# Sums of weight blocks made by accumulating transfers, another order of products, and a branch's products held in DRAM

## The chip, the cores and the metric

The kernel runs on one core of one Trainium2 chip. The metric is the device time of one execution in microseconds (us); lower is better. The time of a kernel is the median of several runs. A profile is one further execution, recorded by the hardware profiler. The engines are named as the profile names them: PE (TensorE), PEld (its weight loads), DVE (VectorE), ACT (ScalarE), POOL (GpSimd) and SP (SyncE, which here only issues DMAs).

## What is computed

One layer of a hybrid encoder trunk on 512 tokens of width 1024, in float32. The core of the reference:

```python
h = _rmsnorm(x, g_pre_mix)
proj = h @ w_in
q, k, v, g, u, sv, a_ret, a_sgu = jnp.split(proj, ...)
y_ret = _retention_branch(q, k, v, g, ret_decay_logit, w_ret_o)     # (layernorm(o) * silu(g)) @ w_ret_o
y_sgu = _sgu_branch(u, sv, sgu_ln_g, sgu_ln_b, w_spatial, b_spatial, w_sgu_o)
merged = jax.nn.sigmoid(a_ret) * y_ret + jax.nn.sigmoid(a_sgu) * y_sgu
x = x + _rmsnorm(merged @ w_out, g_post_mix)
h2 = _rmsnorm(x, g_pre_ffn)
x = x + _rmsnorm(_conv_gated_mlp(h2, w_up, conv_w, conv_b, w_down), g_post_ffn)
```

`_conv_gated_mlp` is a product with `w_up` (1024 x 5632), a convolution over three tokens, a gate (gelu(a) * b) and a product with `w_down` (2816 x 1024).

## The kernel before, in words

**Weights.** All weights are laid out on the host as 146 blocks, `wall`, each 128 x 1024 float32 (512 KB). They stream through the chip in a fixed order of units. SP loads a block into a tile `raw` (a ring of four). Each float32 matrix is then split into two parts of a reduced format: ACT copies it to a high part (`copy`, L79) and DVE subtracts that to give a low part (`tensor_sub`, L86); both go into a ring `w4` of nine slots. PE makes each product as three: high by high, high by low, low by high. `w_get` hands out the next split block, and splits some units ahead (`LOOK`).

**Pairs.** Twenty pairs of blocks (four for `u`, eight for the two gates, eight in the up projection) are multiplied by a scheme with seven products instead of eight, in the manner of Strassen and Winograd. The four quarters of a pair's weight are B11, B12, B21 and B22, each 128 x 512. `w_form` makes the sums T1 = B11 + B12 (DVE, L167), T3 = B12 + B22 (DVE, L168), T2 = T1 + B22 (POOL, L169) and T4 = T2 + B21 (POOL, L171) in `raw` tiles. B12 itself takes part in no product. Each quarter or sum is one unit, split as above, in the order of `FORMS`. The class `Pair` makes the products of 12 matmuls of 128x256 each (L692) into three PSUM banks, b[0] to b[2]: `part1` multiplies B11 (bank 0), B21 (bank 1), T1 with S1 (bank 2) and T2 with S2 (bank 0 again), `part2` T3 with S3 (bank 0), `part3` T4 and B22. S1 to S4 are sums of activations. Where a bank is used again without being cleared, ACT has copied out (L79) or DVE has added what it held before. In the gates, whole blocks (`f_block`, 128x512 matmuls) lie between the parts.

**Down.** The down projection has two halves of nine units of a similar scheme, each with a block `q` (of which 768 columns are used as they are) and a block `t` made from `q`. `w_down` makes the first two columns of 256 of `t` by one DVE addition of a broadcast (L186), and two further ones by L190 and L191, then splits `t`. A pair `q`, `t` gives 42 matmuls of 128x256 (L1058); four whole blocks come between or behind (L1074).

**Stages.** The order on PE, with its time in the profiled execution: the input projections and the retention up to about 217 us; the four `u` pairs to 262 us; the eight gate pairs with whole blocks to 428 us, first four for the retention branch, then four for the SGU branch; the output projection `w_out` (two streamed blocks, then six resident ones, split ahead of use into tiles of their own), norms and transposes to about 500 us; up projection and convolution from 520 us (its first blocks begin before) to 706 us; down projection to the end at 825.7 us, with the last norms in the tail.

**Merging the gates.** For the retention branch `gated_pair` gives products that DVE multiplies by the gate into tiles `r`, eight in all, which stay in SBUF. For the SGU branch DVE multiplies likewise (L805), POOL adds `r` (L806), and the sum is split into `mh` and `ml`, the operands of `w_out`.

Engines work through their queues in order. What a scheduler decided beforehand is fixed in the program; the ring sizes (`raw` four, `w4` nine, `blk` 76 tiles of 128 x 512) say when a buffer may be filled again.

Of the kernel before, what the change touches and what calls it, by code (L numbers as in the profile page):

```python
# [26 lines left out]
NW = 146  # L27
U0, GATE0, GATE1 = 32, 40, 72
LOOK = 4
NBLK = 76  # L30
WARM = 18
RES_OUT = 6
DOWN0 = NW - NF
# [14 lines left out]
def tile_block(ctx: ExitStack, tc, xT, x, wall, par, cs, wsp, bsp, gpost, gffn, out):  # L48
    nc = tc.nc
    sb = ctx.enter_context(tc.tile_pool(name="sb", bufs=1))  # L50
    pp = ctx.enter_context(tc.tile_pool(name="pp", bufs=8, space=bass.MemoryType.PSUM))
    dp_ = ctx.enter_context(tc.tile_pool(name="dp", bufs=1, space=bass.MemoryType.DRAM))
# [3 lines left out]
    def nm(s):  # L56
        uid[0] += 1
        return f"{s}_{uid[0]}"

    def blk(dt=F32, n="blk", shape=(P, S)):  # L60
        return sb.tile(list(shape), dt, tag="blk", bufs=NBLK, name=nm(n))

# [15 lines left out]
    def copy(o, i):  # L78
        nc.scalar.activation(out=o, in_=i, func=AF.Copy)  # L79
# [4 lines left out]
    def split(hi, lo, src):  # L84
        copy(hi, src)
        nc.vector.tensor_sub(lo, src, as32(hi))  # L86
# [2 lines left out]

    RES1 = NW - 22 - 44  # L90
    RES0 = RES1 - RES_OUT
    FORMS = ("B11", "B21", "T1", "T2", "T3", "T4", "B22")
    units = []
    i = 0
    while i < NW:
        pair = [(f, i) for f in FORMS]
        if U0 <= i < GATE0:
            units += pair
            i += 2
        elif GATE0 <= i < GATE1:  # L100
            units += pair[:4] + [("blk", i + 2)] + pair[4:] + [("blk", i + 3)]
            i += 4
        elif i == UP0 + 2 * COUPLES[0][0]:
            for a, b in COUPLES:
                pair = [(f, UP0 + 2 * a) for f in FORMS]
                units += pair[:4] + [("blk", UP0 + 2 * b)] + pair[4:] + [("blk", UP0 + 2 * b + 1)]
            i = UP0 + 2 * COUPLES[-1][1] + 2
        elif i == DOWN0:
            for _ in range(2):
                pairs = [[("q", i + j), ("t", i + j)] for j in range(DP)]  # L110
                whole = [[("blk", i + DP)], [("blk", i + DP + 1)]]
                for u in pairs[:4] + whole[:1] + pairs[4:6] + whole[1:] + pairs[6:] if i == DOWN0 else pairs + whole:
                    units += u
                i += DP + WHOLE // 2
        else:
            units.append(("blk", i))
            i += 1
    w_ready, w_pos, w_held, w_raw = {}, [0, 0], [0], {}

    def raw_tile():  # L120
        return sb.tile([P, 1024], F32, tag="raw", bufs=4, name=nm("raw"))


    AT_64, AT_192 = 16, 48
# [31 lines left out]
    def w_form(form, i):  # L156

        if form == "B11":
            a, b = raw_tile(), raw_tile()
            nc.sync.dma_start(a, wall[i])  # L160
            nc.sync.dma_start(b, wall[i + 1])
            w_raw["B11"], w_raw["B12"] = a[:, :S], a[:, S:]
            w_raw["B22"], w_raw["B21"] = b[:, :S], b[:, S:]
        elif form == "T1":
            t = raw_tile()
            w_raw["T1"], w_raw["T2"], w_raw["T3"], w_raw["T4"] = t[:, :S], t[:, S:], w_raw["B12"], t[:, S:]
            nc.vector.tensor_add(w_raw["T1"], w_raw["B11"], w_raw["B12"])  # L167
            nc.vector.tensor_add(w_raw["T3"], w_raw["B12"], w_raw["B22"])  # L168
            nc.gpsimd.tensor_tensor(out=w_raw["T2"], in0=w_raw["T1"], in1=w_raw["B22"], op=ALU.add)  # L169
        elif form == "T4":  # L170
            nc.gpsimd.tensor_tensor(out=w_raw["T4"], in0=w_raw["T2"], in1=w_raw["B21"], op=ALU.add)  # L171
        w = slot("wf", 0, 1088)
        lo, hi = w[:, AT_64 : AT_64 + S], w[:, S + AT_192 : 2 * S + AT_192]
        split(hi, lo, w_raw[form])
        return hi, lo

    def w_down(form, i):

        if form == "q":
            raw = w_raw["q"] = raw_tile()  # L180
            nc.sync.dma_start(raw, wall[i])
            raw = raw[:, : 3 * 256]
        else:
            b, raw = w_raw["q"], raw_tile()
            two = "p (n c) -> p n c"
            nc.vector.tensor_tensor(  # L186
                out=raw[:, :512].rearrange(two, n=2), in0=b[:, :512].rearrange(two, n=2),
                in1=b[:, None, 768:].to_broadcast([P, 2, 256]), op=ALU.add,
            )
            nc.vector.tensor_add(raw[:, 512:768], raw[:, :256], b[:, 256:512])  # L190
            nc.vector.tensor_add(raw[:, 768:], raw[:, 512:768], b[:, 512:768])  # L191
        w = 768 if form == "q" else 1024
        hi, lo = slot("dh", AT_192, w), slot("dl", AT_192, w)
        split(hi, lo, raw)
        return hi, lo
# [70 lines left out]
    for k in range(KD):  # L266
# [18 lines left out]
        for m in range(8):  # L285
            c = slice(m * P, (m + 1) * P)
# [5 lines left out]
    T0, T1 = slice(0, 256), slice(256, 512)  # L292
# [383 lines left out]
    class Pair:  # L676
# [27 lines left out]
        def part1(self):  # L704
            c0, c1 = self.t
            o = self.product(0, self.x(0, T0), True)
            copy(c0[:, T0], o)
            o = self.product(1, self.x(4, T0), True)
            v.tensor_add(c0[:, T0], o, c0[:, T0])
            self.product(2, self.s("S1"), True)  # L710
            o = self.product(0, self.s("S2"), False)
            copy(c1[:, T0], o)
            if self.scale is not None:
                v.tensor_mul(c0[:, T0], c0[:, T0], self.scale[:, T0])

# [68 lines left out]
    def gated_pair(ah, al, late=None):  # L784
        p = Pair(AF.Sigmoid, lambda: tmp("sig"), None, rbc)
        p.part1()
        if late:
            late.part3()
        o = [f_block(ah, al, KD)]
        p.part2()  # L790
        o.append(f_block(ah, al, KD, p.part3))
        return zip(o, p.t)

    r = []
    for j in range(KD // 2):
        for o, t in gated_pair(ogh, ogl, late if j == 0 else None):
            b = blk(n="r")
            v.tensor_mul(b, o, t)
            r.append(b)
        mix(2 * j)  # L800
        mix(2 * j + 1)
    mh, ml = [], []
    for j in range(KD // 2):
        for i, (o, t) in enumerate(gated_pair(yh, yl)):
            v.tensor_mul(t, o, t)  # L805
            nc.gpsimd.tensor_tensor(out=t, in0=t, in1=r[2 * j + i], op=ALU.add)  # L806
            h_, l_ = blk(F32R, "mh"), blk(F32R, "ml")
            split(h_, l_, t)
            mh.append(h_)
            ml.append(l_)  # L810

    def bcast(src, n):
        t = halves(n)
        for i in range(2):
            nc.gpsimd.dma_start(t[i], src[None, i * S : (i + 1) * S].to_broadcast([P, S]))
        return t
# [229 lines left out]
    def products(m, j, steps={}, look=LOOK):  # L1046
        for n, (unit, at, act) in enumerate(UNITS):
            if n in (0, 3):
                wh, wl = w_get(look)
            if j == 0:  # L1050
                m[n] = ps()
            f = slice(at * 256, (at + 1) * 256)
            ah, al = dforms[j][act]
            for t in range(2):
                c = slice(t * P, (t + 1) * P)
                o = m[n][:, t * 256 : (t + 1) * 256]
                for i, (a_, w_) in enumerate(((ah, wh), (ah, wl), (al, wh))):
                    nc.tensor.matmul(  # L1058
                        o, a_[:, c], w_[:, f], start=j == t == i == 0,
                        stop=j == DP - 1 and i == 2 and n not in (M2, M3, M4), skip_group_check=True,  # L1060
                    )
            steps.get(n, lambda: None)()
# [17 lines left out]
    m = {}  # L1080
    m[M8] = ps()
    late = list(range(EAGER, DP))
    c11, c12, c21, c22 = c4 = [blk(n="c") for _ in range(4)]
    e1, e3, uu, yy = tmp("e1"), tmp("e3"), tmp("uu"), tmp("yy")

    def after6():
# [26 lines left out]
            if j == 5:  # L1113
                copy(c22, m[M8])

    gpf = bcast(gffn, "gpf")
    qn = [small("q", 4, 4) for _ in range(NT)]
    zg = []

# [71 lines left out]
    steps = {M1: lambda: copy(e1, m[M1]), M6: after6, M7: after7}  # L1191
    for j in range(DP):
        products(m, j, steps if j == DP - 1 else {})
        if 1 < j < 2 + NT:
            first_share(j - 2)
    m[M8] = ps()
# [24 lines left out]
def _two(a):  # L1221

    b = _parts(a, 8, P).reshape(4, 2, P, 2, S)
    return np.stack([
        np.concatenate([b[:, 0, :, 0], b[:, 1, :, 0]], -1), np.concatenate([b[:, 1, :, 1], b[:, 0, :, 1]], -1),
    ], 1)


def _up(a):

    for i, _ in COUPLES:
        b, c = a[2 * i].reshape(P, 2, S), a[2 * i + 1].reshape(P, 2, S)
        a[2 * i : 2 * i + 2] = np.stack([
            np.concatenate([b[:, 0], c[:, 0]], -1), np.concatenate([c[:, 1], b[:, 1]], -1),
        ])
    return a

# [83 lines left out]
```

## Time and profile before

| | |
|---|---|
| time, median of 3 runs | 824.46 us (824.05 to 824.6) |
| the profiled execution | 827.49 us |
| its span, first to last instruction | 825.7 us |
| mean granted clock of TensorE | 0.999 |
| bytes moved | 93.24 MB, mean 113 GB/s |

The profile has views for different questions. The busy shares tell what each engine did; the chain of waits follows the work that ended last back to the start; the windows give the busy time of each engine in one stretch; the groups by line give the count, total and mean duration of instructions of one shape; the waits tell which engine waited for what; the timeline lists instructions by their start.

### The profile page before, as it was taken

The page shows a single profiled execution, that of the slowest core. Times are in us where ns is not written, and L with a number is a line of the kernel's source. Part 1 is how long each engine was busy: PE and PEld are TensorE (multiplying, and loading weights), DVE is VectorE, ACT ScalarE, POOL GpSimd, SP SyncE. Part 2 cuts the span into 40 slices and gives each one's busy share as a digit, 9 for nine tenths or more (in the row PEclk, how much of TensorE's full clock was granted, in tenths as well). Part 3 has the DMA queues.
Part 4 walks back from the last instruction along what each step waited for, and adds up shares of the span by engine and source line. Part 5 has one row for each costly group of instructions (what it writes and reads, how often), then busy time and mean ns, then how long its engine had stood idle before and what let it go on. Part 6 is the DMA issues. An engine that isn't in the chain of part 4 may idle for free.

```text
span 825.7 us, 13263 instructions
## 1 busy us (share of the span) xinstructions
PE 815.4 (99%) x5152; PEld 735.0 (89%) x5152; DVE 661.4 (80%) x1101; ACT 440.8 (53%) x771; POOL 101.0 (12%) x102
## 2 busy tenths in 40 slices
PE   9999999999999999999999999999999999999996
PEld 7888888888899999999988898899999998999996
DVE  7489897878797777767765568979899899988967
ACT  6636445546665444444445685556566566544531
POOL 0010000102121111132211211210111200000001
PEclk9999999999999999999999999999999999999999
DMA  8733222212223232222349111322322341233244
GB/s 294 246 116 102 77 77 77 77 52 78 90 102 129 103 102 80 101 101 103 108 166 339 48 55 55 103 102 103 102 103 102 102 154 52 77 115 129 96 147 154
DMA packets 29215, 93.24 MB, mean 113 GB/s; under 512 B 3360, under 2 KB 4000, under 8 KB 29152
## 3 DMA queue, kind: packets, MB, share of 16 engines
q1 hardware_dynamic: 26928, 86.85, 30.2%
q0 software_dynamic: 1360, 4.46, 1.6%
q10 hardware_dynamic: 864, 1.09, 0.4%
q8 instruction: 40, 0.66, 0.3%
q14 instruction: 23, 0.19, 0.1%
HBM read 88.19 MB, written 4.19 MB: 112 GB/s over the span
## 4 chain that ended last, share of the span: by engine, by line
PE 91%; DVE 6%; ACT 1%; issue 1%; DMA 0%; POOL 0%; DVEq 0%; SPq 0%; POOLq 0%; ACTq 0%
PE ps L692 23%; PE ps L217 12%; PE ps L218 12%; PE ps L219 12%; PE ps L1058 8%; PE ps L481 5%; PE ps L480 5%; PE ps L482 5%; PE ps L836 2%; PE ps L837 2%; PE ps L838 2%; PE ps L1074 1%; PE ps L761 1%; DVE fl L86 1%; PE ps L279 1%
## 5 line engine op out<-in xcount | busy, mean ns | idle before, releaser
L86 DVE TENSOR_TENSOR wl<-raw,wh 128x1024 fp32r<-128x1024 f32 (+1 forms) x93 | 109.1, 1182 | 48.9 <-PE ps L692 24.2
L79 ACT ACTIVATE wf<-raw 128x512 fp32r<-128x512 f32 x140 | 85.3, 627 | 102.7 <-PE ps L218 34.0
L86 DVE TENSOR_TENSOR wf<-raw,wf 128x512 fp32r<-128x512 f32 x140 | 111.1, 808 | 23.3 <-ACT wf L79 22.4
L692 PE MATMUL ps<-sh,wf 128*128 128x256 f32 x640 | 119.5, 277 | 0.0
L79 ACT ACTIVATE wh<-raw 128x1024 fp32r<-128x1024 f32 (+2 forms) x95 | 93.3, 993 | 37.4 <-DMA raw<-wall 17.0
L692 PEld LDWEIGHTS ps<-sh,wf 128*128 128x128 f32 x640 | 101.1, 188 | 0.8 <-ACT u L79 0.2
L217 PE MATMUL ps<-h2h,wh 128*128 128x512 f32 (+1 forms) x256 | 92.4, 363 | 0.7 <-ACT h2h L906 0.7
L218 PE MATMUL ps<-h2l,wh 128*128 128x512 f32 (+1 forms) x256 | 92.4, 363 | 0.0
L219 PE MATMUL ps<-h2h,wl 128*128 128x512 f32 (+1 forms) x256 | 92.1, 361 | 0.0
L692 PE MATMUL ps<-sl,wf 128*128 128x256 f32 x320 | 88.8, 278 | 0.0
L480 PE MATMUL ps<-wh,xh 128*128 128x512 f32 x192 | 75.0, 391 | 0.0
L481 PE MATMUL ps<-wl,xh 128*128 128x512 f32 x192 | 74.9, 390 | 0.0
L482 PE MATMUL ps<-wh,xl 128*128 128x512 f32 x192 | 74.8, 390 | 0.0
L169 POOL TENSOR_TENSOR raw<-raw,raw 128x512 f32<-128x512 f32 x20 | 36.2, 1809 | 235.2 <-DVE raw L167 207.8
L1058 PE MATMUL ps<-dl,fh 128*128 128x256 f32 x216 | 60.8, 281 | 0.1
L1058 PE MATMUL ps<-dh,fl 128*128 128x256 f32 x216 | 60.7, 281 | 0.0
L1058 PE MATMUL ps<-dh,fh 128*128 128x256 f32 x216 | 60.7, 281 | 0.0
L692 PEld LDWEIGHTS ps<-sl,wf 128*128 128x128 f32 x320 | 60.0, 188 | 0.6
L219 PEld LDWEIGHTS ps<-h2h,wl 128*128 128x128 f32 x256 | 48.0, 188 | 7.7
L217 PEld LDWEIGHTS ps<-h2h,wh 128*128 128x128 f32 x256 | 47.9, 188 | 7.9 <-ACT h2h L906 1.0
L692 PE MATMUL ps<-xh,wf 128*128 128x256 f32 x288 | 54.2, 278 | 0.0
L218 PEld LDWEIGHTS ps<-h2l,wh 128*128 128x128 f32 x256 | 48.0, 188 | 6.6
(314 smaller groups left out, 2048.9 us busy)
## 6 DMA issues: line engine op xcount, KB each, us to landing
raw<-wall SPq DMA_DIRECT2D x145, 512.0 KB, 3.6
x<-x SPq DMA_DIRECT2D x24, 256.0 KB, 5.9
xT<-xT SPq DMA_DIRECT2D x8, 256.0 KB, 5.4
x<-x POOLq DMA_DIRECT2D x8, 256.0 KB, 2.4
xT<-xT POOLq DMA_DIRECT2D x4, 256.0 KB, 3.6
out<-zg SPq DMA_DIRECT2D x4, 256.0 KB, 2.0
out<-zs ACTq DMA_DIRECT2D x3, 256.0 KB, 3.5
cs<-cs SPq DMA_DIRECT2D x2, 256.0 KB, 4.1
```

Source lines behind the costliest of these rows:

```text
L79: nc.scalar.activation(out=o, in_=i, func=AF.Copy)
L86: nc.vector.tensor_sub(lo, src, as32(hi))
L169: nc.gpsimd.tensor_tensor(out=w_raw["T2"], in0=w_raw["T1"], in1=w_raw["B22"], op=ALU.add)
L217: nc.tensor.matmul(o, ah, bh, start=start, stop=False)
L218: nc.tensor.matmul(o, ah, bl, start=False, stop=False)
L219: nc.tensor.matmul(o, al, bh, start=False, stop=stop)
L480: nc.tensor.matmul(acc[t], xh[k][:, c], wh[:, f], start=k == 0, stop=False)
L481: nc.tensor.matmul(acc[t], xh[k][:, c], wl[:, f], start=False, stop=False)
L482: nc.tensor.matmul(acc[t], xl[k][:, c], wh[:, f], start=False, stop=k == KD - 1)
L692: nc.tensor.matmul(o, w_[:, c], a_, start=first and k == n == 0, stop=k == 3 and n == 2, skip_group_check=True,)
L836: nc.tensor.matmul(o, ah, bh, start=k == 0, stop=False)
L1058: nc.tensor.matmul(o, a_[:, c], w_[:, f], start=j == t == i == 0, stop=j == DP - 1 and i == 2 and n not in (M2, M3, M4), skip_group_check= ...
```

## The change

T1 and T3 are adjacent halves of a new tile `sum` (a ring of two). In the new host layout a pair's first block holds B11 and B21, its second B12 and B22. A plain transfer by SP (the base) fills `sum` with B11 and B12, the first halves of both blocks; an accumulating transfer issued by POOL adds the second block, B12 and B22. The sums of the next pair are issued when the B21 unit of this one is. Of the second block only B22 is loaded beside that, and the free half of its tile takes T2; T4 goes into the half of `sum` that held T1. T2 comes ahead of T1, in the units and in `part1`. In the down projection the broadcast addition is made likewise, one pair ahead. The ring `raw` goes from four tiles to three, `blk` from 76 to 74. The products `r` are stored in DRAM and added back by an accumulating transfer. The broadcast `gpf` of the last norm's weights is issued later, and two tiles `c` lie in another pool.

```diff
-NBLK = 76
+NBLK = 74
...
-    FORMS = ("B11", "B21", "T1", "T2", "T3", "T4", "B22")
+    FORMS = ("B11", "B21", "T2", "T1", "T3", "T4", "B22")
...
-        return sb.tile([P, 1024], F32, tag="raw", bufs=4, name=nm("raw"))
+        return sb.tile([P, 1024], F32, tag="raw", bufs=3, name=nm("raw"))
+
+    def sums(i, first, more):
+        if i not in w_sums:
+            t = w_sums[i] = sb.tile([P, 1024], F32, tag="sum", bufs=2, name=nm("sum"))
+            n = first.shape[1] * first.shape[2]
+            t = t[:, :n].rearrange("p (b c) -> p b c", b=2)
+            nc.sync.dma_start(t, first)
+            nc.gpsimd.dma_start(t, more, accum_op=ALU.add)
+        return w_sums[i]
+
+    def sums_ahead(i):
+        n = w_pairs.index(i) + 1
+        if n < len(w_pairs):
+            (form_sums if w_pairs[n] < DOWN0 else down_sums)(w_pairs[n])
+
+    def form_sums(i):
+        b, w = wall[i : i + 2, :, :S], wall[i + 1].rearrange("p (b c) -> p b c", b=2)
+        return sums(i, b.rearrange("b p c -> p b c"), w)
+
+    def down_sums(i):
+        w = wall[i].rearrange("p (b c) -> p b c", b=4)
+        return sums(i, w[:, 0:2], w[:, 3:4].to_broadcast([P, 2, 256]))
...
         if form == "B11":
-            a, b = raw_tile(), raw_tile()
+            a, b, t = raw_tile(), raw_tile(), form_sums(i)
             nc.sync.dma_start(a, wall[i])
-            nc.sync.dma_start(b, wall[i + 1])
...
+            nc.sync.dma_start(b[:, :S], wall[i + 1, :, S:])
+            w_raw["B11"], w_raw["B21"] = a[:, :S], a[:, S:]
+            w_raw["T1"], w_raw["T3"], w_raw["T4"] = t[:, :S], t[:, S:], t[:, :S]
+            w_raw["B22"], w_raw["T2"] = b[:, :S], b[:, S:]
-        elif form == "T1":
...
-            nc.vector.tensor_add(w_raw["T1"], w_raw["B11"], w_raw["B12"])
-            nc.vector.tensor_add(w_raw["T3"], w_raw["B12"], w_raw["B22"])
+        elif form == "B21":
+            sums_ahead(i)
             nc.gpsimd.tensor_tensor(out=w_raw["T2"], in0=w_raw["T1"], in1=w_raw["B22"], op=ALU.add)
...
         split(hi, lo, w_raw[form])
+        if form == "T1":
+            nc.gpsimd.tensor_tensor(out=w_raw["T4"], in0=w_raw["T2"], in1=w_raw["B21"], op=ALU.add)
...
-            b, raw = w_raw["q"], raw_tile()
-            two = "p (n c) -> p n c"
-            nc.vector.tensor_tensor(
-                out=raw[:, :512].rearrange(two, n=2), in0=b[:, :512].rearrange(two, n=2),
-                in1=b[:, None, 768:].to_broadcast([P, 2, 256]), op=ALU.add,
-            )
+            b, raw = w_raw["q"], down_sums(i)
             nc.vector.tensor_add(raw[:, 512:768], raw[:, :256], b[:, 256:512])
             nc.vector.tensor_add(raw[:, 768:], raw[:, 512:768], b[:, 512:768])
+            sums_ahead(i)
...
-            self.product(2, self.s("S1"), True)
             o = self.product(0, self.s("S2"), False)
             copy(c1[:, T0], o)
+            self.product(2, self.s("S1"), True)
...
-    r = []
+    r = [dp_.tile([P, S], F32, tag=f"r{j}", name=f"r{j}") for j in range(KD)]
...
-            r.append(b)
+            nc.gpsimd.dma_start(r[2 * j + i], b)
...
-            nc.gpsimd.tensor_tensor(out=t, in0=t, in1=r[2 * j + i], op=ALU.add)
+            nc.gpsimd.dma_start(t, r[2 * j + i], accum_op=ALU.add)
...
-    c11, c12, c21, c22 = c4 = [blk(n="c") for _ in range(4)]
+    c11, c12, c21, c22 = c4 = [f(n="c") for f in (blk, blk, tmp, tmp)]
...
-    gpf = bcast(gffn, "gpf")
+    gpf = []
...
+        if j == 0:
+            gpf.extend(bcast(gffn, "gpf"))
```

More of the change, by code (lines that the diff above doesn't have):

```diff
@@ L117, in tile_block @@
             i += 1
+    w_pairs = [i for f, i in units if f in ("B11", "q")]
     w_ready, w_pos, w_held, w_raw = {}, [0, 0], [0], {}
     def raw_tile():
-        return sb.tile([P, 1024], F32, tag="raw", bufs=4, name=nm("raw"))
+        return sb.tile([P, 1024], F32, tag="raw", bufs=3, name=nm("raw"))
+    w_sums = {}
+    def sums(i, first, more):
[16 more added lines that the diff above has]
+        return sums(i, w[:, 0:2], w[:, 3:4].to_broadcast([P, 2, 256]))
     AT_64, AT_192 = 16, 48
@@ L158, in w_form @@
         if form == "B11":
-            a, b = raw_tile(), raw_tile()
+            a, b, t = raw_tile(), raw_tile(), form_sums(i)
             nc.sync.dma_start(a, wall[i])
-            nc.sync.dma_start(b, wall[i + 1])
-            w_raw["B11"], w_raw["B12"] = a[:, :S], a[:, S:]
-            w_raw["B22"], w_raw["B21"] = b[:, :S], b[:, S:]
-        elif form == "T1":
[L165 to L168, printed above, removed]
+            nc.sync.dma_start(b[:, :S], wall[i + 1, :, S:])
[4 more added lines that the diff above has]
+            sums_ahead(i)
             nc.gpsimd.tensor_tensor(out=w_raw["T2"], in0=w_raw["T1"], in1=w_raw["B22"], op=ALU.add)
-        elif form == "T4":
-            nc.gpsimd.tensor_tensor(out=w_raw["T4"], in0=w_raw["T2"], in1=w_raw["B21"], op=ALU.add)
         w = slot("wf", 0, 1088)
@@ L792, in gated_pair @@
         return zip(o, p.t)
-    r = []
+    r = [dp_.tile([P, S], F32, tag=f"r{j}", name=f"r{j}") for j in range(KD)]
     for j in range(KD // 2):
-        for o, t in gated_pair(ogh, ogl, late if j == 0 else None):
+        for i, (o, t) in enumerate(gated_pair(ogh, ogl, late if j == 0 else None)):
             b = blk(n="r")
             v.tensor_mul(b, o, t)
-            r.append(b)
+            nc.gpsimd.dma_start(r[2 * j + i], b)
         mix(2 * j)
@@ L1224, in _two @@
     return np.stack([
-        np.concatenate([b[:, 0, :, 0], b[:, 1, :, 0]], -1), np.concatenate([b[:, 1, :, 1], b[:, 0, :, 1]], -1),
+        np.concatenate([b[:, 0, :, 0], b[:, 0, :, 1]], -1), np.concatenate([b[:, 1, :, 0], b[:, 1, :, 1]], -1),
     ], 1)
@@ L1233, in _up @@
         a[2 * i : 2 * i + 2] = np.stack([
-            np.concatenate([b[:, 0], c[:, 0]], -1), np.concatenate([c[:, 1], b[:, 1]], -1),
+            np.concatenate([b[:, 0], b[:, 1]], -1), np.concatenate([c[:, 0], c[:, 1]], -1),
         ])
```

## The prediction

> **What bounds the kernel now.** I read the share of busy time first, then the chain that ended last, then the windows by stage, and then the list of what TensorE waited for.
>
> ```profile
> span 825.7 us, 13263 instructions
> PE 815.4 (99%) x5152; PEld 735.0 (89%) x5152; DVE 661.4 (80%) x1101; ACT 440.8 (53%) x771; POOL 101.0 (12%) x102
> PE 91%; DVE 6%; ACT 1%; issue 1%; DMA 0%; POOL 0%; DVEq 0%; SPq 0%; POOLq 0%; ACTq 0%
> 600.00:680.00 80.00, 80.00 (x514) 72.29 (x513) 74.93 (x117) 49.56 (x84) 8.83 (x6) 1.00 0.35 119
> 735.00:808.00 73.00, 73.00 (x622) 73.00 (x621) 56.02 (x89) 32.40 (x50) 0.54 (x1) 1.00 0.35 122
> 808.00:826.00 18.00, 10.34 (x88) 10.13 (x87) 12.86 (x33) 3.62 (x15) 2.50 (x4) 0.93 0.51 175
> ```
>
> TensorE is busy for 815.4 of 825.7 us. The window rows give length, then busy time of PE, PEld, DVE, ACT and POOL, the clock, the DMA share and GB/s. In the up stage (600 to 680) and the down stage (735 to 808) PE is busy for every microsecond, although DVE is at 94% in the first. Of the 10.3 us in which PE isn't busy, 7.7 (18.00 less 10.34) lie in the tail behind 808, which the change doesn't shorten, and most of the rest before the first block. The change takes no matmul away, so what it can gain is what PE waits for in between:
>
> ```profile
> PE ps L624 <- DVE o L615: 0.3, 1, 0.3
> PEld ps L624 <- DVE o L615: 0.6, 1, 0.6
> PEld ps L692 <- ACT c L79: 0.4, 1, 0.4
> PEld ps L1058 <- DVE dl L86: 0.3, 1, 0.3
> ```
>
> (microseconds in total, times, longest). There is one thing more, the step of TensorE itself, from one start of a 128x256 product to the next:
>
> ```profile
> 219.36 0.28 PE L692 MATMUL ps<-sh,wf 128*128 128x256 f32 x1
> ...
> 222.08 0.28 PE L692 MATMUL ps<-xh,wf 128*128 128x256 f32 x1
> ...
> 222.31 0.39 PE L692 MATMUL ps<-xh,wf 128*128 128x256 f32 x2
> 222.72 0.39 PE L692 MATMUL ps<-sh,wf 128*128 128x256 f32 x1
> 222.94 0.28 PE L692 MATMUL ps<-sl,wf 128*128 128x256 f32 x1
> 223.00:262.00 39.00, 39.00 (x330) 39.00 (x330) 35.60 (x55) 24.66 (x45) 9.66 (x7) 1.00 0.35 122
> 222.28 0.39 ACT L79 ACTIVATE u<-ps 128x256 f32<-128x256 f32 x1 [0.73 <-PE ps L692]
> ```
>
> Two products (24 matmuls) lie between 219.36 and 222.08: 113.3 ns each. At 222.31 to 222.94 three steps take 0.63 us instead of 0.34, a stall of 0.29, because product S3 goes into the bank which the copy at 222.28 is still emptying. Behind it, to the end of the u stage, 39 us hold 330 matmuls: 118.2 ns each at the same granted clock of 1.00. The stall seems to leave PE in a slower step from which it doesn't come back.
>
> **The change, part by part.** *T1 and T3 by transfers.* What DVE loses:
>
> ```profile
> L167 DVE TENSOR_TENSOR raw<-raw 128x512 f32<-128x512 f32 x20 | 13.8, 688 | 1.5 <-DMA raw<-wall 1.4
> L168 DVE TENSOR_TENSOR raw<-raw,raw 128x512 f32<-128x512 f32 x20 | 17.1, 853 | 1.0 <-DMA raw<-wall 0.7
> L186 DVE TENSOR_TENSOR raw<-raw 128x512 f32<-128x512 f32 x18 | 12.4, 688 | 8.5 <-DMA raw<-wall 8.4
> ```
>
> 13.8 + 17.1 + 12.4 = 43.3 us of DVE, or 1.54 us for each pair of weights and 0.69 for each down pair. On the path it is worth only the waits above. The o products (L615) before the u stage have an L167 and an L168 among them, 1.54 us together, more than the 0.3 us (PE) to 0.6 us (its loads) of wait: I count 0.4 gained. The `dl` wait of 0.3 and the `c` wait of 0.4 stand behind DVE too; I count half of each, 0.35, since ACT's share stays.
>
> *T2 ahead of T1.* In the first u pair S1's product (12 matmuls, though the changed kernel's order on PE draws 4 of them ahead of S2) now lies between S2's copy and S3, so the 0.29 us stall should go. Gains so far: 0.4 + 0.35 + 0.29, about 1.0 us. Whether the slow step goes with the stall is a case of its own below.
>
> The same exchange has a price. S2 adds into bank b0, and must wait until ACT has copied the B11 product out of it. Before, B21 and S1 lay between; now B21 alone, 12 x 113.3 ns = 1.36 us. Where S1 starts now, S2 will want to start:
>
> ```profile
> 281.90 0.28 PE L692 MATMUL ps<-sh,wf 128*128 128x256 f32 x1
> 282.28 0.36 ACT L79 ACTIVATE sig<-ps 128x256 f32<-128x256 f32 x1
> 646.12 0.28 PE L692 MATMUL ps<-sh,wf 128*128 128x256 f32 x1
> 646.89 0.37 ACT L79 ACTIVATE c<-ps 128x256 f32<-128x256 f32 x1
> ```
>
> At 281.90 the copy would be late by 282.64 - 281.90 = 0.74 us, at 646.12 by 647.26 - 646.12 = 1.14 us. These are the first and the last of the five late ones among the 16 gate and up pairs; an estimate of 0.6 for each of the three between makes 3.7 us; the lower bound is nothing, if ACT's queue, which is late here because it waits on DVE, moves up by the 1.54 us per pair that DVE gains. In the first gate pair the new order also puts five S1 matmuls (0.57 us) ahead of S2. I take the nearer to nothing, 1.0 us, since 1.54 exceeds every lateness but not all of it sits ahead of the copy.
>
> A stall may bring the slow step here as well. The rule of the Trainium skill speaks against that ("TensorE: Matmul & The Clock Gate", "LDWEIGHTS (loading the stationary operand)": a load takes about its columns over 1.2, an estimate of 107 ns for 128, below the step). By that page a stall would cost itself alone; the 118.2 ns of the trace differ, and the trace decides.
>
> *The new transfers.* A pair moves 512 KB base (SP) and 512 KB accumulating (POOL), with half a block less: 1 MB becomes 1.75 MB. The next rows have what is near:
>
> ```profile
> 432.00:460.00 28.00, 28.00 (x128) 23.24 (x127) 16.77 (x26) 13.45 (x26) 3.41 (x6) 1.00 0.72 262
> raw<-wall SPq DMA_DIRECT2D x145, 512.0 KB, 3.6
> x<-x POOLq DMA_DIRECT2D x8, 256.0 KB, 2.4
> gpf<-gffn POOLq DMA_DIRECT2D x2, 256.0 KB, 4.0
> out<-zg SPq DMA_DIRECT2D x4, 256.0 KB, 2.0
> raw<-wall SPq DMA_DIRECT2D x1, 256.0 KB, 4.8
> ```
>
> Where DMA is at 0.72 and 262 GB/s, PE loses nothing; at 0.3 a stage nearly doubled stays below that. So volume costs nothing. No accumulating transfer is in this trace; I bound 512 KB by 3.6 below and twice that, 7.2, above (it reads its target too). Base and sum in series are 7 to 11 us. The fastest pairs, in the u stage, take 84 matmuls of 118.2 ns, 9.9 us, and the two `sum` tiles make the cycle two pairs, 19.9 us, of which the use of a tile (T2 to T4) leaves about half: 10 us, just enough in the middle of the bounds; the gate and up pairs have whole blocks between them and more room. The accumulating issue stands on POOL ahead of T2 of the current pair and holds it until the base has landed; on SP the base stands ahead of block loads, and holds them until its `sum` tile is free, with three `raw` tiles in place of four. The same room covers both; if it is gone, T2 or the next block is late by what is over. The later broadcast of `gpf` (4.0 us) still has a pair of time before its first reader: nothing.
>
> *Down pairs.* Here the room is small. With two `sum` tiles the base of pair n+2 waits until t of pair n is split. The chain is base + accumulating sum + two adds + split:
>
> ```profile
> L190 DVE TENSOR_TENSOR raw<-raw,raw x18: 415/419/426, 679.9 to 793.1; 128x256 f32<-128x256 f32 x18
> L79 ACT ACTIVATE dh<-raw 128x1024 fp32r<-128x1024 f32 x18 | 19.1, 1059 | 21.2 <-DVE raw L191 12.9 <-PE ps L1058 5.1 <-PE ps L219 1.6
> L86 DVE TENSOR_TENSOR dl<-raw,dh 128x1024 fp32r<-128x1024 f32 x18 | 22.0, 1222 | 3.8 <-ACT dh L79 2.4 <-PE ps L1058 1.2
> 740.00:800.00 60.00, 60.00 (x512) 60.00 (x511) 49.44 (x81) 27.41 (x43) 0.54 (x1) 1.00 0.36 124
> ```
>
> 2 x 0.42 + 1.06 + 1.22 = 3.1 us, with base 2.0 to 4.8 and sum 2.4 to 8 (twice 4.0): 7.5 to 15.9. I take base 2.8 (an estimate, nearer the unloaded 2.0 at a DMA share of 0.35) and sum 4.0: 9.9 us. A pair has 42 matmuls, which at 60 us for 512 of them take 4.9 us; two pairs are 9.8. So it just holds, and a lead of a pair, some 5 us, cushions it: nothing lost in the likeliest case. If the sum comes later, the add waits for it on DVE with the splits `dl` and `fl` of the next blocks queued behind it, and PE's loads wait for those.
>
> *Gated products off the chip.* Eight POOL additions of 1.47 us become eight stores and eight accumulating loads:
>
> ```profile
> L806 POOL TENSOR_TENSOR sig<-sig,r 128x512 f32<-128x512 f32 x8 | 11.6, 1465 | 36.4 <-DVE sig L805 36.4
> 429.43 1.28 POOL L806 TENSOR_TENSOR sig<-sig,r 128x512 f32<-128x512 f32 x1 [2.07 <-DVE sig L805]
> 430.74 0.63 ACT L79 ACTIVATE mh<-sig 128x512 fp32r<-128x512 f32 x1 [2.17 <-POOL sig L806]
> 431.28 4.28 ACT L79 ACTIVATE wh<-raw 128x512 fp32r<-128x512 f32 x8
> ```
>
> The last sum then takes 2.4 to 4.5 us instead of 1.28, so `mh` and the eight resident splits queued behind it on ACT move by some 2 to 3 us, to end near 438 to 439 instead of 435.6. The first resident isn't wanted before 438.5: two streamed blocks of 24 matmuls come first, from 428 on, at 28.00 us for 128 of them (0.219 each, 5.25 a block). With three `raw` tiles instead of four the last resident is loaded only when the first is split; it may come 0 to 1.2 us late. I take 0.3.
>
> **Sum.** On the profiled execution, 827.49 us (span 825.7): -1.0 +1.0 +0.3 = +0.3, so 827.8. The median of the runs, 824.46, lies 3.0 below the profiled one; the same +0.3 there is 824.8. About 0.2%, 1.65 us, is what a measurement of this kernel can tell from no change.
>
> **Rivals.** *The u stage keeps the fast step (faster).* If the stall at 222.4 goes and no other follows, 330 matmuls gain 118.2 - 113.3 = 4.9 ns each: 1.6 us. With the other terms 824.8 - 1.6 = 823.2, and with the copies in time (1.0 us less) 822.2. For it: the step changes just at the stall. Against it: in the faster step B21 covers less, and one new stall undoes it.
>
> *The down sums become the bound (slower).* Above about 10.7 us of chain the cushion is used up: over some twelve pairs each loses half of what is over 9.8, less 5 us. At 11 us that is 12 x 0.6 - 5 = 2.2 us, at 12 us 8.2. The point is an accumulating sum of 4.8 us, against 4.0 of the nearest POOL row. I price it at 6, giving 830.8. Against it: POOL's 2.4. The Trainium skill speaks for it ("SBUF — State Buffer", "SBUF: two separate sides": DVE in its two-port mode keeps GpSimd from writing the descriptors of its transfers). By that page the sums would be issued late; no trace here shows it, and the spread of 2.4 to 4.0 us would agree.
>
> *The copies stay as late as they are (slower).* +3.7 instead of +1.0, and five stalls each followed by some 60 matmuls at 5 ns more, 1.5 us: 824.8 + 2.7 + 1.5 = 829.0. For it: the rows at 282 and 646. Against it: DVE's relief.
>
> *The transfers only move work that was hidden, with no wait gone or new:* 824.5, inside my forecast.
>
> **How the numbers follow.** Forecast (terms cancel, 822.9 to 826.1): 0.40. Fast step in u with copies in time, below 822.8: 0.21. Down sums: 0.20. Late copies: 0.14. A mishap elsewhere, such as residents late or the start's loads crowded, over 1.65 us: 0.05. Faster 0.21, same 0.40, slower 0.39. The range runs from 822.2 to 831.0: it leaves out half of the down case's upper part and the lower half of the fast one. The likeliest case's own range is 822.9 to 826.1.
>
> **What would show it.** PE rows at the first u pair: S3 without a gap, and 223 to 262 with 344 matmuls in 39 us (fast step) or 330 (slow). Waits of `L712` products for ACT copies of 128x256 tell the price of the exchange. In the down stage a wait of DVE for the `sum` transfers that grows from pair to pair, with PE waiting for `dl`, is the slower rival. DVE should be at about 618 us. A gain above 3 us, or a loss in the gate stage, would mean that I missed something.

## The result and the profile after

The changed kernel takes 854.21 us (median of 4 runs, 852.11 to 861.4) against 824.25 us for the kernel before: 30.0 us more, a ratio of 1.038 with a 95% interval of 1.0315 to 1.0444. That is slower, and outside the range of 822.2 to 831.0. The profiled execution took 861.4 us.

The page of the changed kernel, its span and busy shares:

```profile
span 859.6 us, 13409 instructions
PE 828.0 (96%) x5152; PEld 743.2 (86%) x5152; DVE 614.3 (71%) x1043; ACT 437.8 (51%) x771; POOL 151.3 (18%) x148
```

DVE lost 47 us, a little more than the 43.3 counted, and it bought nothing: PE is busy for 12.6 us more with the same 5152 matmuls, and idle for 21 us more. The waits of PE of the changed kernel (us in total, times, longest) say for whom:

```profile
PE ps L1078 <- DVE dl L86: 12.2, 10, 3.5
PE ps L1078 <- ACT dh L79: 3.6, 2, 2.0
PE ps L712 <- ACT sig L79: 2.7, 1, 2.7
PE ps L238 <- DVE h2l L929: 1.6, 2, 1.0
```

L1078 is the down projection's product (L1058 before). The windows of the changed kernel place the loss (length, busy time and count of PE, PEld, DVE, ACT, POOL, clock, DMA share, GB/s):

```profile
220.00:267.00 47.00, 47.00 (x382) 45.94 (x381) 36.00 (x57) 27.76 (x51) 14.62 (x12) 1.00 0.70 184
418.00:432.00 14.00, 11.28 (x62) 9.96 (x61) 7.42 (x11) 4.86 (x9) 0.86 (x1) 0.88 0.58 174
432.00:520.00 88.00, 85.72 (x486) 74.75 (x485) 58.69 (x111) 56.58 (x136) 12.74 (x20) 1.00 0.39 129
520.00:600.00 80.00, 80.00 (x504) 71.86 (x503) 61.17 (x96) 43.58 (x75) 20.42 (x12) 1.00 0.50 141
600.00:680.00 80.00, 80.00 (x519) 72.35 (x518) 64.77 (x107) 49.93 (x86) 22.57 (x11) 1.00 0.45 132
713.00:761.00 48.00, 48.00 (x409) 47.97 (x408) 35.04 (x59) 23.33 (x34) 7.26 (x6) 1.00 0.61 160
761.00:800.00 39.00, 28.73 (x214) 26.55 (x212) 23.09 (x42) 13.47 (x28) 7.27 (x7) 0.96 0.57 139
800.00:840.00 40.00, 32.98 (x222) 31.79 (x223) 16.98 (x23) 10.61 (x12) 4.81 (x4) 0.83 0.57 146
```

One of the same windows in the kernel before:

```profile
761.00:800.00 39.00, 39.00 (x333) 39.00 (x333) 32.61 (x56) 17.75 (x32) 0.54 (x1) 1.00 0.39 134
```

In the u stage and the up stage PE is full, though more bytes move there (184 GB/s against 113 from 220 to 267 us, 141 against 106 from 520 to 600). It loses mainly at two places: at 418 to 432 us, and in the down stage from 761 us on, where 214 matmuls stand in 39 us that had 333 in the kernel before (and 347 with DVE making the sums, below). The clock falls there too: 0.83 from 800 to 840. A third, smaller loss lies between 432 and 520 us, where PE is idle for 2.3 us, 1.6 of them for `h2l`.

How the down stage comes to wait is read in the chain that ended last, of the changed kernel, between 750 and 775 us (start, length, what):

```profile
752.75 4.89 DMA sum<-wall
757.64 0.02 issue
757.66 0.04 POOLq L133
757.70 0.61 issue
758.31 4.43 DMA sum<-wall
762.74 0.02 issue
762.77 0.43 DVE sum L209
763.20 0.02 issue
763.22 0.03 DVE sum L210
...
763.57 1.23 DVE dl L86
```

This is the loop that the prediction named: the base, 4.9 us; 0.7 us from its landing to POOL's issue; the accumulating transfer, 4.4 us from that issue to landing; the adds and a split, which frees a tile for the next base. The DMA issues of the changed kernel in 700 to 845 us give the medians from issue to landing:

```profile
sum<-wall SPq DMA_DIRECT2D x16, 256.0 KB, 4.0
sum<-wall POOLq DMA_DIRECT2D x16, 256.0 KB, 5.3
```

With the prediction's 3.1 us for adds and split, 4.0 + 0.7 + 5.3 + 3.1 = 13.1 us, against 9.8 us of PE for two pairs. The prediction had 2.8 + 4.0 + 3.1 = 9.9.

### The profile page after: what moved, and what is told of

The parts are those of the page before. It is cut to its first block, busy times and chain, and to the rows that moved or that the text cites. A ratio compares the mean times of both kernels' runs of the same rounds, so it can differ in the third digit from the quotient of the medians.

```text
span 859.6 us, 13409 instructions
## 1 busy us (share of the span) xinstructions
PE 828.0 (96%) x5152; PEld 743.2 (86%) x5152; DVE 614.3 (71%) x1043; ACT 437.8 (51%) x771; POOL 151.3 (18%) x148
## 3 DMA queue, kind: packets, MB, share of 16 engines
q0 software_dynamic: 10928, 23.86, 14.6%
## 4 chain that ended last, share of the span: by engine, by line
PE 74%; DVE 8%; DMA 8%; issue 5%; ACT 3%; POOL 1%; DVEq 0%; ACTq 0%; POOLq 0%
PE ps L712 21%; PE ps L237 11%; PE ps L238 11%; PE ps L239 11%; DMA sum<-wall 6%; PE ps L501 5%; PE ps L500 5%; PE ps L502 5%; PE ps L1078 2%; DVE dl L86 2%; PE ps L1094 1%; DMA sig<-r 1%; DMA gpf<-gffn 1%; DVE fl L86 1%; PE ps L781 1%
## 5 line engine op out<-in xcount | busy, mean ns | idle before, releaser
L86 DVE TENSOR_TENSOR wl<-raw,wh 128x1024 fp32r<-128x1024 f32 (+1 forms) x93 | 106.5, 1154 | 64.2 <-PE ps L712 36.9
L133 POOL DMA_DIRECT2D sum<-wall x38 | 39.8, 1046 | 291.8 <-DMA sum<-wall 81.3
L86 DVE TENSOR_TENSOR wf<-raw,wf 128x512 fp32r<-128x512 f32 x80 | 56.7, 723 | 37.1 <-ACT wf L79 36.7
L79 ACT ACTIVATE wf<-raw 128x512 fp32r<-128x512 f32 x80 | 49.1, 625 | 61.2 <-PE ps L238 42.9
L1078 PE MATMUL ps<-dl,fh 128*128 128x256 f32 x216 | 63.6, 295 | 7.8 <-DVE dl L86 7.8
L1078 PE MATMUL ps<-dh,fh 128*128 128x256 f32 x216 | 63.6, 295 | 5.1 <-ACT dh L79 3.6
L1078 PE MATMUL ps<-dh,fl 128*128 128x256 f32 x216 | 62.9, 291 | 0.0
L79 ACT ACTIVATE wf<-sum 128x512 fp32r<-128x512 f32 x60 | 37.6, 627 | 45.6 <-PE ps L712 31.3
L79 ACT ACTIVATE dh<-sum 128x1024 fp32r<-128x1024 f32 x18 | 19.1, 1059 | 73.4 <-DVE sum L210 63.1
```

The costliest lines, as they stand in the source:

```text
L133: nc.gpsimd.dma_start(t, more, accum_op=ALU.add)
L1078: nc.tensor.matmul(o, a_[:, c], w_[:, f], start=j == t == i == 0, stop=j == DP - 1 and i == 2 and n not in (M2, M3, M4), skip_group_check= ...
```

## The experiments

**Undoing the down sums, r, or both.** `e1_down_dve`: the part of `w_down` that makes the sum.

```diff
-            b, raw = w_raw["q"], down_sums(i)
+            b, raw = w_raw["q"], sb.tile([P, 1024], F32, tag="sum", bufs=2, name=nm("sum"))
+            nc.vector.tensor_tensor(out=raw[:, :512]..., in0=b[:, :512]..., in1=b[:, None, 768:]..., op=ALU.add)
...
-            sums_ahead(i)
```

> The changed kernel with one part undone: in the down projection the broadcast sum is made by a DVE addition again (into the same two sum tiles), so that no transfer makes a sum there. Theory A (the loop of two sum tiles is the bound in the down stage: base 3 to 5, POOL's issue 1.2, landing 3.2 to 5.4, adds 0.8, split 2.3, together 12 to 13 us against 9.8 of PE for two pairs): the down stage takes 113 us again as before, the time falls by 20 to 27 us to about 830, and PE waits for dl only some tenths. Rival B (the doubled DMA traffic, or a TensorE clock lowered throughout, slows PE in all stages): only the share of the down stage's 9 MB goes, a few us, and the clock stays below 0.99.

833.21 us, ratio 1.010 (1.0083 to 1.0117): 21.0 us of the 30 gone. Its windows have PE full at clock 1.00 where the changed kernel was short:

```profile
761.00:800.00 39.00, 39.00 (x347) 39.00 (x346) 34.06 (x59) 19.49 (x35) 0.56 (x1) 1.00 0.44 138
```

`e2_r_chip` keeps `r` in SBUF and adds it by POOL; `e3_both` does both.

```diff
-            nc.gpsimd.dma_start(r[2 * j + i], b)
+            r.append(b)
...
-            nc.gpsimd.dma_start(t, r[2 * j + i], accum_op=ALU.add)
+            nc.gpsimd.tensor_tensor(out=t, in0=t, in1=r[2 * j + i], op=ALU.add)
```

> The changed kernel with one part undone: the products r stay in SBUF and POOL adds them, as before. Theory C (the accumulating loads of r, 4 to 8 us each instead of 1.3, hold ACT's queue at mh, with it the raw ring, and PE's product S2 waits 2.9 us at 422 with a lowered clock behind it, and h2l is late at 478 to 482): the stretch from 418 to 520 us gets back to that of before, 6 to 8 us less, about 847. Rival D (three raw tiles instead of four make that stretch late): it stays late by at least half of that, about 851.

> The changed kernel with both undone, the down sums and r; what stays is T1 and T3 by transfers in the u, gate and up pairs, T2 ahead of T1, and three raw tiles. Theories A and C together: 823 to 825, since the u stage is 0.8 us shorter in the profile of the changed kernel and the gate and up pairs lose some tenths at the copies out of bank 0. Rival B: 830 or more, as these pairs hold most of the added traffic.

`e2_r_chip`: 853.13 us, 1.1 less than the changed kernel, within the spread of runs of either (849.9 to 861.4). `e3_both`: 828.97, above the 823 to 825 expected, and 4.2 less than `e1_down_dve`. That r should explain PE's wait at 422 us (theory C) was wrong: the wait is still 2.5 us. How much of the 4.2 us is r itself stays open. In `e1_down_dve` the clock is 0.70 from 425 to 430 us, behind a wait of 2.9 us, and in `e3_both` it is 1.00; but `e2_r_chip`, with r on the chip too, has 0.66 there. Only kernels with r in DRAM, though not all of them, have PE wait for `h2l` between 460 and 500 us: 1.6 us in the changed kernel, 1.0 in `e14_base` below, none in `e1_down_dve`.

**The order alone.** `e4_order` puts T2 and S2 ahead in the kernel before.

```diff
-            self.product(2, self.s("S1"), True)
             o = self.product(0, self.s("S2"), False)
             copy(c1[:, T0], o)
+            self.product(2, self.s("S1"), True)
```

> The kernel before with the order alone changed: T2 ahead of T1 in the units and S2 ahead of S1 in part1; all sums on DVE and POOL as before. It asks what the exchange costs without DVE's relief. Theory of the prediction's third rival (the copy out of bank 0 is late by 0.3 to 1.1 us in five pairs): 1 to 4 us slower, 825.5 to 828. Rival (the first u pair loses its stall and the u stage keeps the step of 113 ns): 0.5 to 2 us faster.

831.74 us, ratio 1.0093 (1.0071 to 1.0116): 7.7 us slower, more than expected. The waits of PE of this kernel:

```profile
PE ps L692 <- ACT c L79: 4.8, 4, 2.6
```

Four times PE waits in the up stage for the copy out of bank 0, as the prediction's rival had it; 2.6 us of it in the first pair, and behind that the clock falls, to 0.79 from 524 to 532 us. `e6_s1first` asks the converse: `e3_both` with the old order.

> The kernel with both undone, and the old order too: T1 ahead of T2 in the units, S1 ahead of S2 in part1. What stays is T1 and T3 by transfers. Theory G (the exchange makes the copy's lateness felt): the wait at 422 shrinks from 2.6 to about 1.2 us and the stalls in the up stage go; but the 222 us stall of the kernel before is back and the u stage keeps the slow step (about 1 us more there); together 826 to 828. Theory E or F alone: the wait at 422 stays near 2.6 less 1.4, as the same 1.36 us of cover returns, so this run tells the exchange's whole price and not which of E and F holds.

828.64 us beside 828.97 of `e3_both`; by the ratios, 1.0044 beside 1.0066, with intervals that overlap. Without DVE's relief the exchange costs 7.7 us; with it, nothing clear of noise (`e15_best` below asks nearly the same and finds 0.6 us).

**The wait at 422 us.** In `e3_both` the chain runs through a block load, and ACT's timeline has the copy behind the splits of that block:

```profile
415.52 7.43 DMA raw<-wall
```

```profile
422.97 2.10 ACT L79 ACTIVATE wh<-raw 128x512 fp32r<-128x512 f32 x3 [2.93 <-DMA raw<-wall]
424.98 0.36 ACT L79 ACTIVATE sig<-ps 128x256 f32<-128x256 f32 x1
```

The load took 7.43 us. The sum of the first up pair, which isn't read before 503 us, is made at the same time: its base went out at 409.7 us, and its accumulating transfer of 512 KB, issued at 413.8, took 8.1 us. `e5_raw4` gives the ring a fourth tile and takes two `blk` tiles for it.

> The kernel with both undone (DVE makes the down sums, r stays on the chip) and four raw tiles again instead of three (two blk tiles less). It asks what makes PE wait 2.6 us for the bank 0 copy at 422 us. Theory E (the ring of three: the resident blocks are loaded late, their splits stand ahead of the copy in ACT's queue): the wait goes, and the kernel falls from 829.0 to about 825. Rival F (the sum of the first up pair is made at that moment, its accumulating transfer took 8.05 us there and the block beside it 7.4): the block is late all the same, and it stays at 828 to 829. Rival G (the exchange of S1 and S2, which takes 1.36 us of cover away): the wait shrinks by at most half.

840.18 us. The wait at 422 is gone, but the kernel waits 5.3 us for `u` at 238 us, and elsewhere: two `blk` tiles fewer is a change of its own, and the run separates nothing. `e10_upsum` issues the sum later in the code.

> The kernel with both undone (DVE makes the down sums, r on the chip, three raw tiles, the new order), in which the sum of the first up pair is issued with that pair's own first unit, not from the last gate pair a hundred microseconds ahead. Theory F (this transfer of 1 MB collides at 409 to 422 us with the loads of the resident blocks, which took 5.4 and 7.4 us there): the wait of 2.6 us at 422 goes, and the time falls from 829.0 to 825 to 826.5 (the sum is then not ahead at 520 us, which may cost some tenths). Theory E (the ring of three raw tiles alone): it stays at 828 to 829.

830.85 us. A miss: the order of transfers on SP's queue stayed as it was, so the run tested nothing. (By its ratio, 1.0069, it is as fast as `e3_both`, 1.0066; the medians differ by 1.9 us.) `e13_uplate` binds the up pairs' base transfers behind the loads of x on that queue.

```diff
-            nc.sync.dma_start(t, first)
+            with tc.issue_after(late_x[-1]) if i >= UP0 else ExitStack():
+                nc.sync.dma_start(t, first)
```

> Again the question of e10, whose edit in the code left the order of the transfers as it was. Here the base transfers of the up pairs are bound behind the loads of x on SP's queue, so that the 1 MB for each of the first two up pairs isn't moved between 409 and 422 us; all else as in e3 (DVE makes the down sums, r on the chip, three raw tiles, the new order). Theory F (collision with the resident blocks' loads): the wait of 2.6 us at 422 us goes, 829 becomes 825 to 827. Theory E (three raw tiles alone): the wait stays above 2 us and the time at 828 to 830.

825.60 us, ratio 1.0025 (1.0014 to 1.0037): 3.4 us less than `e3_both`. ACT's timeline of this kernel:

```profile
418.80 2.11 ACT L79 ACTIVATE wh<-raw 128x512 fp32r<-128x512 f32 x3 [0.47 <-DMA raw<-wall]
420.81 0.36 ACT L79 ACTIVATE sig<-ps 128x256 f32<-128x256 f32 x1
```

The same block is there 4.2 us earlier, and PE no longer waits, with three raw tiles and the new order as before. The three block loads that go out there, two us apart in both kernels, land in 4.0 us in the median instead of 5.4: it was the collision (theory F).

**Why the down sums are late.** `e7_sum3` has three `sum` tiles (and two `blk` fewer), `e11_two` also issues two pairs ahead. `e8_plain` replaces the accumulating transfer of the down stage by a plain one, `e14_base` leaves it out.

> The changed kernel with three sum tiles instead of two (two blk tiles less), all else as changed. Theory A, as a loop: base, accumulating transfer, adds and split together are 12 to 13 us, and with three tiles the budget is three pairs, 14.7 us: the down stage loses only a few tenths, and the time falls by about 20 us to 832 to 836. Rival H (not the ring but the throughput of POOL's accumulating transfers, or of DMA in the down stage, is the bound): nothing changes, 850 or more.

> The changed kernel with three sum tiles, as before, and in the down stage the sums issued two pairs ahead instead of one. If the chain's latency is what counts, the down stage gets back near 113 us and the time falls from 847 to 832 to 837. If the ring of q tiles (each held until its sum has landed and been added to) or SP's and DVE's order set the pace, it stays at 843 or more.

> The changed kernel, but the down stage's second transfer is a plain one of the same bytes by POOL (it overwrites instead of adding, so the down sums lack their first part). Theory A says that two latencies in series are too long: base 3 to 5, POOL's issue 1.2 and the landing. If adding itself is the slow part, the landing falls from 3.2 to 5.4 us after the issue to the 2 to 3.4 us of POOL's plain loads in the kernel before, 1 to 2 us of the loop, and about a quarter to half of the 21 us goes: 842 to 849. If a POOL transfer of small pieces costs the same without the addition, it stays at 850 or more.

> The changed kernel without the second transfer of the down sums: the base alone fills the sum tile (the down sums lack their second part). It leaves two sum tiles, three raw tiles, and base and block loads in the same order on SP. If the second latency (POOL's issue and landing, 4.4 to 7 us) is what the ring of two can't bear, the chain is 8 us against 9.8 and the down stage is whole: 832 to 835, as with DVE's addition. If the ring or SP's order itself is too tight, it stays above 840.

847.26, 849.20, 843.76 and 834.23 us. The base alone leaves the two rings and SP's order as they are, and the down stage is whole again; windows of `e14_base`:

```profile
761.00:800.00 39.00, 39.00 (x333) 39.00 (x332) 29.34 (x52) 19.43 (x34) 0.56 (x1) 1.00 0.54 168
```

So the second transfer is what the loop can't bear: 20 of the 21 us. About half of that, 10.5 us, is the adding itself. In `e8_plain` the same bytes, not added, land sooner:

```profile
sum<-wall SPq DMA_DIRECT2D x18, 256.0 KB, 2.9
sum<-wall POOLq DMA_DIRECT2D x18, 256.0 KB, 3.9
```

3.9 us against 5.3; the base too, the same in both kernels, lands in 2.9 us instead of 4.0. A third tile gives back 7 us only (expected: 20), and a longer lead nothing. The simple picture, a latency divided by the number of tiles, is therefore not enough: by it the chain of `e8_plain`, 2.9 + 0.7 + 3.9 + 3.1 = 10.6 us, would cost next to nothing, and the kernel is 9.5 us slower than `e14_base`. What the picture lacks can be seen in the timelines of the changed kernel (ACT, DVE and SP in order of time):

```profile
755.48 1.06 ACT L79 ACTIVATE dh<-sum 128x1024 fp32r<-128x1024 f32 x1 [3.28 <-DVE sum L210]
762.77 0.42 DVE L209 TENSOR_TENSOR sum<-sum,raw 128x256 f32<-128x256 f32 x1 [6.59 <-DMA sum<-wall]
763.57 1.22 DVE L86 TENSOR_TENSOR dl<-sum,dh 128x1024 fp32r<-128x1024 f32 x1
763.82 1.06 ACT L79 ACTIVATE dh<-sum 128x1024 fp32r<-128x1024 f32 x1 [6.07 <-DVE sum L210]
764.81 0.33 SPq L132 DMA_DIRECT2D sum<-wall  x1
```

The low split at 763.57 starts before the high part of the sum just finished (763.82), so it is that of the pair before, whose high part was done at 756.5. It stood behind the adds, which waited for the transfer; only its end frees that tile for the next base, at 764.81. From one base to the next into the same tile the issues of the last eleven turns give 15.3 us on average, 13.0 in `e8_plain` and 11.3 in `e14_base`, where PE doesn't wait. Half the difference for each of eleven pairs is some 22 and 9 us, close to the 20 and 9.5 between the runs. That the order on DVE is what lengthens the turn is read from the trace; no run changed it. A `q` tile is held until its sum has landed (L210 reads both) and DVE's adds wait with splits behind them; which of these sets the pace with three tiles stays open.

**What the good part is worth.** `e9_u1` is the kernel before with the exchange in the first u pair alone; `e12_kick` adds to it eight transposes ahead of the down stage; `e15_best` is `e13_uplate` with the old order in all pairs but that one.

> The kernel before with the exchange (T2 and S2 ahead of T1 and S1) in the first u pair alone; nothing else. The prediction's theory of the step: the stall of 0.29 us at 222 goes and with it what sets the slow step, so that all 386 matmuls of the u stage take 113.3 ns: 2.1 us faster, about 822.3. Rival (the step is set by something else than that stall, or another stall of a tenth sets it again in the second pair): 0.3 to 0.9 us faster, no more.

> The kernel of the first u pair's exchange with eight more transposes of 128x128 on PE ahead of the down stage's first product; their result is overwritten. It asks whether the step of 117.8 ns of the down stage (113.3 in several runs behind a stall) is a matter of how PE enters it. If the transposes set the fast step there: about 950 matmuls by 4.5 ns, 4.3 us less, less 0.9 us for the transposes: 3 us below the kernel without them. If not: 0.9 us above it.

> e13 with the old order of S1 and S2 in all pairs but the first u pair: what the parts of the change that cost nothing could give together. If the collision was the one cost left, and the fast step in the u stage is kept: 822 to 824. If the T1 and T3 transfers have a price of their own (three raw tiles, waits for blocks): 826 to 829.

822.75, 824.80 and 824.97 us; ratios 0.9981 (0.997 to 0.9993), 1.0005 (0.9993 to 1.0017) and 1.0013 (1.0001 to 1.0026). `e9_u1` beats the kernel before by 1.7 us; `e12_kick` loses 2.1 us against `e9_u1`, where 3 less or 0.9 more was expected. `e15_best` lies between the two cases expected of it. It differs from `e13_uplate` by the old order alone, 0.6 us. Against `e9_u1` it has T1 and T3 made by transfers and the smaller rings: by the ratios 2.6 us slower. So the part of the change that was left to help costs something, although DVE has less to do. The windows of `e9_u1`, in the u stage and the down stage:

```profile
223.00:246.00 23.00, 23.00 (x205) 23.00 (x204) 21.82 (x34) 15.19 (x29) 6.16 (x4) 1.00 0.34 115
740.00:800.00 60.00, 60.00 (x532) 60.00 (x531) 49.05 (x79) 28.89 (x45) 0.54 (x1) 1.00 0.40 128
```

112.2 ns a matmul (23.00 over 205) where the kernel before had 118.2, and 532 matmuls in the 60 us that held 512. In its trace the u stage is 1.4 us shorter and the down stage 3.0; but the profiled execution of the kernel before is 3 us above its median, so that the 1.7 us can't be divided between them. Behind 246 us a small stall sets the slower step again (10.00 us for 87, 114.9, with the matmuls that overlap the edges; a step of 118.9 in the timeline). In `e12_kick` the down stage has the fast step from 705 us on (in the other sixteen profiles it starts with the slow one, and `e9_u1` has the fast one from about 732 without transposes). Around 762 us PE then waits for DVE, 1.0 us in all, and the slow step follows.

```profile
740.00:755.00 15.00, 15.00 (x135) 15.00 (x134) 10.72 (x17) 6.94 (x8) 0.00 (x0) 1.00 0.32 107
770.00:800.00 30.00, 30.00 (x257) 30.00 (x257) 24.25 (x43) 12.77 (x14) 0.00 (x0) 1.00 0.44 151
```

## Why the prediction was wrong

**The step that failed** is the one headed "Down pairs": it held that the chain "just holds" and counted nothing. The mechanism was described, and stands as a rival with a chance of 0.20, but its terms were mis-sized: base 2.8 (measured 4.0), sum 4.0 (5.3), and 0.7 us between the base's landing and POOL's issue was left out. The base was taken near the unloaded row, 2.0, although the row of the same kind of transfer at 4.8 stood beside it; the sum near a plain transfer, although nothing said that adding is free, and `e8_plain` shows that it costs 1.4 us. The rival's own formula with 13.1 us gives 12 x 1.65 - 5 = 14.8 us, some 6 short of the 20 to 21 measured (`e14_base`, `e1_down_dve`); the rival was priced at 6, between the 2.2 and 8.2 that it gives for 11 and 12 us. Two things it had no term for. One is the low split that stands on DVE behind the next pair's adds: the prediction let the splits behind a late add delay PE, but not the tile, and a turn took 15.3 us. The other is the clock, which falls behind such waits: 0.04 of 39 us and 0.17 of 40 are lost by the windows, at most 8.4 us (an estimate, as if PE were busy throughout). Whether DVE kept POOL from issuing, the other reason given for that rival, no run tests; the 0.7 us from landing to issue were all the delay in the turn shown.

**"So volume costs nothing"** failed at one place: the mean DMA share was the wrong measure. The first up pair's sum is made some 90 us ahead of its use, beside the loads that are urgent just then: 3.4 us (`e13_uplate` against `e3_both`).

**"Gated products off the chip"** was counted at 0.3 and cost up to 4 (`e3_both` against `e1_down_dve`, part of it by the clock). An accumulating load of r took 4.2 us in the median of eight, inside the bounds of 2.4 to 4.5, but the longest took 7.9, and ACT waited up to 4.0 us for one with all its later work behind.

**The copies out of bank 0** (1.0 us) were about right, and for the reason given: with DVE's additions in place the exchange costs 7.7 us (`e4_order`), without them nothing clear of noise (`e6_s1first`) or 0.6 us (`e15_best`). The third rival's 5.2 us, 3.7 for copies and 1.5 for slow steps, fell short of the 7.7.

**The waits before the u stage** (0.4 us) didn't go: the changed kernel still has them, 0.6 and 0.3 where the kernel before had 0.3 and 0.3.

```profile
PE ps L625 <- DVE o L635: 0.6, 1, 0.6
PE ps L644 <- DVE o L635: 0.3, 1, 0.3
```

So taking DVE's additions away doesn't end them.

**The fast step** of the u stage was right: `e9_u1` has it, and the changed kernel too, until a stall at 235 us; by this the u stage is 0.7 us shorter there. In the trace of `e9_u1` it is 1.4 us shorter, near the 1.6 that the rival gave; the forecast itself had put nothing for it.

The sum, from medians: second transfer in the down stage 20, r with the clock about 4, the collision 3.4, and some 2 us left in `e13_uplate` (ratio 1.0025), of which `e15_best` gives 0.6 to the order; the rest no run took apart.

## What to carry to other kernels

A transfer that adds takes two latencies in series and a wait between two queues; before it replaces an engine's 0.7 us, put base, hand-over, sum and use in a row against the time that its ring gives, at the loaded durations and not the best ones, and ask what else waits in the queue behind the use. A prefetch is work of its own at the moment when it runs: ask which urgent load it meets. And where TensorE is nearly full, look at its step as well as its waits.

## What the runs showed of the hardware

The adding costs time in the transfer: 5.3 us against 3.9 for the same 256 KB, from POOL's issue to landing; the issue alone takes 1.2 us against 0.7. It also moves in smaller pieces. The queue with POOL's transfers (q0 on the pages) has 10928 packets in the changed kernel and 7472 in `e8_plain`, for 23.86 MB in both: 192 more for each of the 18 transfers. Whether that is why it takes longer is not shown.

Behind a wait of some microseconds TensorE can run at half its clock for some more. In the timeline of the changed kernel:

```profile
764.84 0.38 PE L1078 MATMUL ps<-dl,fh 128*128 128x256 f32 x1 [3.48 <-DVE dl L86]
...
766.53 0.41 PE L1078 MATMUL ps<-dh,fl 128*128 128x256 f32 x1
766.74 0.41 PE L1078 MATMUL ps<-dh,fh 128*128 128x256 f32 x1
766.95 0.41 PE L1078 MATMUL ps<-dl,fh 128*128 128x256 f32 x1
```

From 766.5 on the steps are 0.21 us instead of 0.113, 1.7 us after a wait of 3.5. The Trainium skill has this ("TensorE: Matmul & The Clock Gate", "What's actually happening": the clock goes to half after an idle window of about 3.4 us). In the trace the half clock lasts about as long as that window: 0.81 over the 9 us from 761 to 770 makes 3.4 us at half. But shorter waits were enough: one of 2.4 us at 422 us in `e10_upsum` (clock 0.66 from 425 to 430 us), while one of 2.5 at the same place in `e3_both` left it at 1.00. So the length of a wait alone doesn't decide here.

A stall of some tenths can set the step of 128x256 matmuls with changing weights to 113.3 or to 118 ns, in either direction, until the next disturbance. What comes before can steer it: from 224 to 234 us in the u stage it is 113.3 ns in 14 of the 15 profiles with the exchange in the first u pair (118.9 in `e7_sum3`), and 118.9 in the two without (the kernel before, `e6_s1first`). What sets it is not known.
